# Turning the state columns of several chunks to rows with one transpose each: a two-layer decoder step on one Trainium2 core

## The chip, the cores and the metric

The kernel runs on one core of a Trainium2 chip, in one launch. The metric is the device time of one execution in microseconds; a median of several runs is given. The engines are called as in the profile: PE (TensorE; PEld is its weight load), DVE (VectorE), ACT (ScalarE), POOL (GpSimd) and SP (SyncE, which here only issues DMAs).

## What is computed

One inference step of two layers over 512 new prompt rows and 8 sequences of 4 decode rows, 544 rows in all, in float32. Layer 0 mixes tokens by a convolution module, layer 1 by stick-breaking attention; each layer ends in a feed-forward block with a gate that is convolved over 3 rows. Cut to what the change touches:

```python
D_MODEL, SEQ, DEC_BATCH, DEC_SEQ = 1024, 512, 8, 4
D_FF, CONV_WIDTH, FFN_CONV_WIDTH = 2816, 31, 3

def conformer_conv(h, past, ...):
    a, gate = jnp.split(h @ w_in + b_in, 2, axis=-1)
    glu = a * jax.nn.sigmoid(gate)
    ext = jnp.concatenate([past, glu], axis=1)
    y = causal_dwconv(ext, w_dw, b_dw)
    y = jax.nn.silu(layer_norm(y, ln_g, ln_b))
    return y @ w_out + b_out, ext[:, -(CONV_WIDTH - 1):]

def conv_ffn(h, past, w_gate, w_up, w_dw, b_dw, w_down):
    g = h @ w_gate
    ext = jnp.concatenate([past, g], axis=1)
    g_conv = causal_dwconv(ext, w_dw, b_dw)
    out = (jax.nn.silu(g_conv) * (h @ w_up)) @ w_down
    return out, ext[:, -(FFN_CONV_WIDTH - 1):]
```

The second results are outputs of the kernel, the states for the next step. The convolution's state is the last 30 rows of `glu` for the prompt, and for each decode sequence its 26 newest past rows and its 4 new ones, 1024 channels each. The feed-forward state is the last 2 rows of the gate for the prompt and for each of the 8 sequences, 18 rows of 2816 channels in each layer.

## The kernel before

Activations lie transposed: channels on the 128 partitions in chunks (8 chunks of the model's 1024 channels, 22 of the feed-forward's 2816), rows along the free axis. So a state that is to be written as rows has to be turned. A float32 product is made of three PE matmuls on rounded parts: weights split into `whi` and `wlo` (ACT casts, L369; DVE subtracts, L372), inputs into high and low parts (`XH`/`XL`, or `HH`/`HL` for the hidden layer of the feed-forward block). The first 272 or 256 rows and the rest are separate streams.

Each stage is written as a list of operations in `Plan`, with an engine, an assumed cost and the buffers read and written. `Plan.run` simulates them and so fixes the order of instructions on every engine; on the chip each engine runs its own list in order and waits where data are not there. Buffers are rings: a tile can be taken again when its last user is done. PSUM has eight banks, `acc` four, `tr` and `av` two each.

**Feed-forward block, `ffn` (once a layer).** The 22 chunks are taken in four passes, `PASSES = ((0, 4), (4, 6), (10, 6), (16, 6))` (first chunk, count). A pass makes gate products (into `acc` banks, emptied by ACT and DVE into a buffer `G`, two in a ring), convolves and multiplies with the up products, and leaves the pass's hidden chunks in `HH` and `HL`. The down products of a pass (L1343 to L1345, added to `xT` on DVE at L1634) run among the gate products of the next pass; those of the last pass follow the block (L459 to L461). `taps` has POOL copy a chunk's 18 state columns from `G` to `SF[:, f, :]` (L1491, L1492). When a pass ends, `state_rows` takes up to four chunks at a time: one PE transpose each (L1645) into one PSUM bank, side by side as [18, 128 x chunks], one ACT copy (L1652) to a tile of the ring `h` (four tiles, used for hidden chunks too), and two stores on POOL's queue, 2 rows of the prompt and 16 of the decode sequences (L1648, L1649). `psum2` takes the banks `tr` and `av` in turn.

**Convolution.** `state(False)` turns the last 30 prompt rows, which lie in `tail_p` [128, 8 chunks, 30], `state(True)` the 32 new decode rows in `glu_s` [128, 8, 32]: for each half of four chunks four transposes (L1117) into an `av` bank and one ACT copy (L1120) into a tile `prod` (two in a ring, which `ffn_rows` fills next). SP stores the prompt's rows with one DMA (L1128) and the decode rows with eight (L1126). Around them in the plan stand the last products of the convolution's output (L700 to L702), whose result DVE adds to `xT` (L1196), ACT squares (L1177) and POOL or DVE sums (L1184); L1207 turns that sum into a mean on PE.

## Time and profile before

| | |
|---|---|
| median of 3 runs | 1292.23 us (1292.02 to 1292.42) |
| profiled execution | 1294.01 us |
| its span on the core | 1292.0 us |
| clock granted to PE over the span | 0.998 of full |
| DMA engines' packets | 142.39 MB, mean 110 GB/s |

The page lists busy time by engine, then 40 slices of the span, then the chain that ended last, then the costliest groups. Each line of the timeline view has start, duration, engine, line of the kernel, operation, output and inputs, shapes and count; in brackets stand the idle time of the engine just before and what ended it. Matmul durations are latencies of pipelined instructions; successive ones overlap, so prices are read from the distance between starts.

The stages of the span, from the view by windows (busy us of PE, DVE and ACT):

| stretch, us | PE | DVE | ACT |
|---|---|---|---|
| 200 to 260 (end of convolution, start of block 0) | 59.86 | 45.98 | 31.63 |
| 260 to 640 (block 0, start of attention) | 377.18 | 294.42 | 189.52 |
| 640 to 900 (attention) | 258.14 | 168.30 | 160.96 |
| 900 to 1280 (block 1, final norm) | 379.02 | 301.41 | 195.79 |

### The profile page before, as it was taken

The numbers are of one execution on the slowest core, as the hardware profiler recorded it, in microseconds if no ns is written. First come the engines' busy times: TensorE is split into PE (matmuls) and PEld (weight loads), VectorE is DVE, ScalarE is ACT, GpSimd is POOL, SyncE is SP. The second block draws the span as 40 slices with busy tenths as digits, with TensorE's granted clock in tenths as the row PEclk, the third lists the DMA queues.
The fourth block names the chain that finished last, engine by engine and source line by source line (L and its number), as shares of the span: only waits on it lengthen the run. The fifth ranks groups of instructions, "written<-read, shape, count | busy, mean of one in ns | idle before, by whom it ended". The sixth has DMA issues, their size and how long they took to land.

```text
span 1292.0 us, 26645 instructions
## 1 busy us (share of the span) xinstructions
PE 1274.7 (99%) x10908; PEld 1220.0 (94%) x10908; DVE 981.1 (76%) x1671; ACT 718.5 (56%) x1448; POOL 158.5 (12%) x301
## 2 busy tenths in 40 slices
PE   9999999999999999999999999999999999999997
PEld 8997789999999999999988988889999999999997
DVE  6899876988977887768356586756988987886864
ACT  6596574545654455445356587754645655455453
POOL 4000013111011010000142123100111011011000
PEclk9999999999999999999999999999999999999999
DMA  7464333123233233143544446333133233233221
GB/s 214 123 184 134 88 99 114 34 83 115 91 106 102 83 99 115 58 141 135 180 148 130 139 129 175 110 116 98 50 100 101 92 105 115 66 116 92 81 76 70
DMA packets 119308, 142.39 MB, mean 110 GB/s; under 512 B 5588, under 2 KB 110312, under 8 KB 118915
## 3 DMA queue, kind: packets, MB, share of 16 engines
q1 hardware_dynamic: 109871, 111.89, 28.0%
q0 software_dynamic: 9024, 28.78, 7.2%
q8 instruction: 86, 1.41, 0.5%
q14 instruction: 35, 0.29, 0.1%
q10 hardware_dynamic: 292, 0.02, 0.0%
HBM read 129.34 MB, written 12.18 MB: 110 GB/s over the span
## 4 chain that ended last, share of the span: by engine, by line
PE 92%; DVE 3%; issue 2%; ACT 1%; DMA 1%; DVEq 0%; POOL 0%; ACTq 0%; POOLq 0%; SPq 0%
PE acc L1545 5%; PE acc L1543 5%; PE acc L1544 5%; PE acc L700 4%; PE acc L701 4%; PE acc L702 4%; PE av L1343 3%; PE acc L460 3%; PE acc L459 3%; PE acc L461 3%; PE av L1344 3%; PE av L1345 3%; PE tr L1343 3%; PE tr L1344 3%; PE tr L1345 3%; PE tr L1545 3%
## 5 line engine op out<-in xcount | busy, mean ns | idle before, releaser
L372 DVE TENSOR_TENSOR wlo<-raw,whi 128x1024 fp32r<-128x1024 f32 (+2 forms) x245 | 257.4, 1052 | 45.0 <-ACT whi L369 43.2
L369 ACT CAST whi<-raw 128x1024 fp32r<-128x1024 f32 (+2 forms) x245 | 223.5, 914 | 115.3 <-PE tr L1344 21.7
L700 PE MATMUL acc<-XH,whi 128*128 128x288 f32 (+1 forms) x384 | 114.4, 298 | 0.0
L701 PE MATMUL acc<-XL,whi 128*128 128x288 f32 (+1 forms) x384 | 110.8, 288 | 0.0
L702 PE MATMUL acc<-XH,wlo 128*128 128x288 f32 (+1 forms) x384 | 110.3, 287 | 0.0
L1970 PE MATMUL acc<-XH,whi 128*128 128x256 f32 (+1 forms) x264 | 82.8, 314 | 0.6 <-ACT XH L2275 0.6
L1543 PE MATMUL acc<-TH,whi 128*128 128x272 f32 x288 | 82.9, 288 | 0.0
L1545 PE MATMUL acc<-TH,wlo 128*128 128x272 f32 x288 | 82.8, 288 | 0.0
L1544 PE MATMUL acc<-TL,whi 128*128 128x272 f32 x288 | 82.7, 287 | 0.0
L1579 ACT COPY G<-acc 128x272 f32<-128x272 f32 (+1 forms) x72 | 26.7, 371 | 95.2 <-PE acc L1545 95.2
L1971 PE MATMUL acc<-XL,whi 128*128 128x256 f32 (+1 forms) x264 | 76.2, 289 | 0.1
L1972 PE MATMUL acc<-XH,wlo 128*128 128x256 f32 (+1 forms) x264 | 75.9, 287 | 0.0
L700 PEld LDWEIGHTS acc<-XH,whi 128*128 128x128 f32 x384 | 72.3, 188 | 2.8 <-issue 1.6
L1343 PE MATMUL av<-HH,whi 128*128 128x288 f32 (+1 forms) x256 | 74.5, 291 | 0.0
L1344 PE MATMUL av<-HL,whi 128*128 128x288 f32 (+1 forms) x256 | 74.1, 290 | 0.0
L1345 PE MATMUL av<-HH,wlo 128*128 128x288 f32 (+1 forms) x256 | 73.9, 289 | 0.0
L1343 PE MATMUL tr<-HH,whi 128*128 128x256 f32 (+1 forms) x256 | 73.4, 287 | 0.0
L1344 PE MATMUL tr<-HL,whi 128*128 128x256 f32 (+1 forms) x256 | 73.3, 286 | 0.0
L1345 PE MATMUL tr<-HH,wlo 128*128 128x256 f32 (+1 forms) x256 | 72.9, 285 | 0.0
L701 PEld LDWEIGHTS acc<-XL,whi 128*128 128x128 f32 x384 | 72.3, 188 | 0.4
L702 PEld LDWEIGHTS acc<-XH,wlo 128*128 128x128 f32 x384 | 72.2, 188 | 0.0
L1484 DVE SCALAR_TENSOR_TENSOR cv<-G,fprm,cv 128x560 f32<-128x560 f32 x88 | 69.4, 796 | 0.5
(409 smaller groups left out, 4417.4 us busy)
## 6 DMA issues: line engine op xcount, KB each, us to landing
raw<-in_ffn_w_gate_dram SPq DMA_DIRECT2D x22, 1024.0 KB
raw<-in_ffn_w_up_dram SPq DMA_DIRECT2D x22, 1024.0 KB
raw<-in_ffn_w_down_dram SPq DMA_DIRECT2D x24, 768.0 KB
raw<-in_attn_w_qkv_dram SPq DMA_DIRECT2D x12, 1024.0 KB
raw<-in_conv_w_in_dram POOLq DMA_DIRECT2D x6, 1024.0 KB, 6.3
rep<-glu SPq DMA_DIRECT2D x36, 142.0 KB
raw<-in_conv_w_out_dram POOLq DMA_DIRECT2D x4, 1024.0 KB, 6.3
raw<-in_ffn_w_down_dram SPq DMA_DIRECT2D x8, 512.0 KB
```

Source lines behind the costliest of these rows:

```text
L369: act.copy(hi[:, k, :], src[:, k])
L372: dve.tensor_tensor(lo[:, k, :], src[:, k], hi[:, k, :], op=ALU.subtract)
L700: pe.matmul(o, hi[:, k, :], XH[:, k, c0:c0 + n], start=(k == 0), stop=False)
L701: pe.matmul(o, hi[:, k, :], XL[:, k, c0:c0 + n], start=False, stop=False)
L702: pe.matmul(o, lo[:, k, :], XH[:, k, c0:c0 + n], start=False, stop=(k == NC - 1))
L1343: pe.matmul(o, hi[:, j + k, :], xh, start=(start and k == 0), stop=False, **kw)
L1344: pe.matmul(o, hi[:, j + k, :], xl, start=False, stop=False, **kw)
L1345: pe.matmul(o, lo[:, j + k, :], xh, start=False, stop=(stop and k == len(xs) - 1), **kw)
L1543: pe.matmul(o, hi[:, j + k, :], xh, start=(start and k == 0), stop=False, **kw)
L1544: pe.matmul(o, hi[:, j + k, :], xl, start=False, stop=False, **kw)
L1545: pe.matmul(o, lo[:, j + k, :], xh, start=False, stop=(k == 3), **kw)
L1970: pe.matmul(o, hi[:, k, :], XH[:, k, c0:c0 + n], start=(k == 0), stop=False)
```

## The change

A transpose turns [128 partitions, n columns] to [n, 128]. The new code lets the n columns be those of several chunks that lie side by side. In the feed-forward block a pass's part of `SF` (18 x 4 or 18 x 6 columns) is filled in the order row by row, within a row chunk by chunk (`mine`), so one transpose gives [72 or 108, 128], with the 2 prompt rows' pieces first. One ACT copy of 128 elements a partition follows, and two stores of pieces of 128 channels. There are no smaller groups any more: one PSUM bank, one tile `h`, one copy and two stores a pass. In the convolution four chunks of `tail_p` (120 columns) or `glu_s` (128 columns) are turned at once, the two halves into one bank, side by side; one ACT copy of 256 elements takes both, and four DMAs on SP store them, one for each place of a chunk within its half.

```diff
@@ -1107,26 +1107,24 @@
 
     def state(new):
         m = NS if new else PAST
-        row = buf("ctmp", "prod", [P, D], 2)
-        for half in range(2):
-            pt = psum("av")
-
-            def turn(half=half, pt=pt):
-                for j in range(4):
-                    c = half * 4 + j
-                    pe.transpose(pt()[:m, j * P:(j + 1) * P], glu_s[:, c, :] if new else tail_p[:, c, :], ident)
-
-            plan.op("pe", 0.45, turn, r=[("new" if new else "tail", half * 4 + j) for j in range(4)], w=[pt])
-            plan.op("act", 0.56, lambda half=half, pt=pt: act.copy(row()[:m, half * 512:(half + 1) * 512], pt()[:m, :]),
-                    r=[pt], w=[row])
+        src = (glu_s if new else tail_p).rearrange("p c t -> p (c t)")
+        row, pt = buf("ctmp", "prod", [P, D], 2), psum("av")
+
+        def turn():
+            for half in range(2):
+                pe.transpose(pt()[:4 * m, half * P:(half + 1) * P], src[:, 4 * half * m:4 * (half + 1) * m], ident)
 
         def store():
-            if new:
-                for b in range(NB):
-                    nc.sync.dma_start(out=sc_s[0, b, PAST - NI:PAST, :], in_=row()[b * NI:(b + 1) * NI, :])
-            else:
-                nc.sync.dma_start(out=sc_p[0, 0], in_=row()[:m, :])
-
+            for j in range(4):
+                r = row()[j * m:(j + 1) * m, :2 * P].rearrange("t (h d) -> t h d", h=2)
+                if new:
+                    dst = sc_s[0, :, PAST - NI:PAST, :].rearrange("b t (h j d) -> b t h j d", h=2, j=4)
+                    nc.sync.dma_start(out=dst[:, :, :, j, :], in_=r)
+                else:
+                    nc.sync.dma_start(out=sc_p[0, 0].rearrange("t (h j d) -> t h j d", h=2, j=4)[:, :, j, :], in_=r)
+
+        plan.op("pe", 0.22, turn, r=[("new" if new else "tail", c) for c in range(NC)], w=[pt])
+        plan.op("act", 0.33, lambda: act.copy(row()[:4 * m, :2 * P], pt()[:4 * m, :2 * P]), r=[pt], w=[row])
         plan.op("sp", 3.0, store, r=[row])
 
 
@@ -1488,9 +1486,11 @@
             plan.op("act", 0.2, lambda: act.activation(
                 smp(s(), SEQ, T), s()[:, SEQ:].rearrange("p (b t) -> p b t", b=NB)[:, :, 2:], AF.Silu), r=["table"], w=[s])
             gs = lambda: g()[:, 2 + SEQ:].rearrange("p (b t) -> p b t", b=NB)
-            plan.op("pool", 0.2, lambda: pool.tensor_copy(SF[:, f, 0:2], g()[:, SEQ:SEQ + 2]), r=[g], w=[("SF", f)])
+            k0, nk = next(x for x in PASSES if x[0] <= f < sum(x))
+            mine = SF[:, k0:k0 + nk, :].rearrange("p f r -> p (f r)").rearrange("p (r f) -> p f r", f=nk)[:, f - k0, :]
+            plan.op("pool", 0.2, lambda: pool.tensor_copy(mine[:, 0:2], g()[:, SEQ:SEQ + 2]), r=[g], w=[("SF", f)])
             plan.op("pool", 0.2, lambda: pool.tensor_copy(
-                SF[:, f, 2:18].rearrange("p (b t) -> p b t", b=NB), gs()[:, :, 4:6]), r=[g], w=[("SF", f)])
+                mine[:, 2:18].rearrange("p (b t) -> p b t", b=NB), gs()[:, :, 4:6]), r=[g], w=[("SF", f)])
 
         def plain_pair(f2, s0, k0):
 
@@ -1636,22 +1636,21 @@
                 used(slots[c - c2])
 
         def state_rows(k0, nk):
-            for f0 in range(k0, k0 + nk, 4):
-                m = min(4, k0 + nk - f0)
-                pt, row = psum2(), buf(None, "h", [P, T], H_BUFS)
-
-                def turn(f0=f0, m=m, pt=pt):
-                    for j in range(m):
-                        pe.transpose(pt()[:18, j * P:(j + 1) * P], SF[:, f0 + j, :], ident)
-
-                def store(f0=f0, m=m, row=row):
-                    pool.dma_start(out=sf_p[l, 0][:, f0 * P:(f0 + m) * P], in_=row()[0:2, :m * P])
-                    pool.dma_start(out=sf_s[l].flatten_outer_dims()[:, f0 * P:(f0 + m) * P], in_=row()[2:18, :m * P])
-
-                plan.op("pe", 0.11 * m, turn, r=[("SF", f0 + j) for j in range(m)], w=[pt])
-                plan.op("act", acost(m * P), lambda m=m, pt=pt, row=row: act.copy(row()[:18, :m * P], pt()[:18, :m * P]),
-                        r=[pt], w=[row])
-                plan.op("pool", 1.4, store, r=[row])
+            pt, row = psum2(), buf(None, "h", [P, T], H_BUFS)
+            m = 18 * nk
+
+            def store():
+                r = row()[:m, :P]
+                fs = slice(k0 * P, (k0 + nk) * P)
+                for dst, lo, n in ((sf_p[l, 0], 0, 2), (sf_s[l].flatten_outer_dims(), 2, 16)):
+                    pool.dma_start(out=dst[:, fs].rearrange("r (f c) -> r f c", f=nk),
+                                   in_=r[lo * nk:(lo + n) * nk])
+
+            plan.op("pe", 0.11, lambda: pe.transpose(
+                pt()[:m, :P], SF[:, k0:k0 + nk, :].rearrange("p f r -> p (f r)"), ident),
+                r=[("SF", f) for f in range(k0, k0 + nk)], w=[pt])
+            plan.op("act", acost(P), lambda: act.copy(row()[:m, :P], pt()[:m, :P]), r=[pt], w=[row])
+            plan.op("pool", 1.4, store, r=[row])
 
 
         first = slot_no[0]
```

The planner sees other costs and fewer operations, so some orders move. On PE, at the end of the convolution, the rows around the state transposes (av, tr, acc: PSUM banks; sqa: the sum of squares). Before:

```order
L1117 MATMUL av_178_2647<-ident_61,tail_p_84 30x128 x4
L1117 MATMUL av_179_2654<-ident_61,tail_p_84 30x128 x4
L700 MATMUL acc_182_2666<-XH_73,whi16_1444 128x288
L701 MATMUL acc_182_2666<-XL_74,whi16_1444 128x288
L702 MATMUL acc_182_2666<-XH_73,wlo16_1445 128x288
...
L1207 MATMUL tr_183_2676<-sqa_166_2483,mean_m_66 128x256
L1117 MATMUL av_184_2680<-ident_61,glu_s_88 32x128 x4
L1117 MATMUL av_186_2689<-ident_61,glu_s_88 32x128 x4
```

and now:

```order
L1115 MATMUL av_178_2647<-ident_61,tail_p_84 120x128 x2
L1115 MATMUL av_179_2651<-ident_61,glu_s_88 128x128 x2
L700 MATMUL acc_183_2667<-XH_73,whi16_1444 128x288
L701 MATMUL acc_183_2667<-XL_74,whi16_1444 128x288
L702 MATMUL acc_183_2667<-XH_73,wlo16_1445 128x288
...
L1205 MATMUL tr_184_2682<-sqa_166_2483,mean_m_66 128x256
```

The transposes of `glu_s` moved from behind the mean of squares (L1207, in the new kernel L1205) to the place beside those of `tail_p`, ahead of the same six matmuls (three are shown).

On ACT, at the end of the feed-forward block of layer 0 (h: ring of rows and hidden chunks; raw, whi: weights; sqa: the next norm's squares). Before:

```order
L369 CAST whi131_7009<-raw47_6892 128x768
L1596 CAST HH0_3038<-h_395_6906 128x544
L1652 COPY h_401_7026<-av_399_7017 18x512
L1652 COPY h_402_7029<-tr_400_7022 18x256
L369 CAST whi132_7034<-raw48_6963 128x768
L1596 CAST HH0_3038<-h_397_6942 128x544
```

and now:

```order
L369 CAST whi131_6969<-raw47_6852 128x768
L1596 CAST HH0_3021<-h_389_6866 128x544
L1652 COPY h_394_6979<-av_393_6977 108x128
L369 CAST whi132_6986<-raw48_6923 128x768
L1596 CAST HH0_3021<-h_391_6902 128x544
```

The two copies became one at the same place, between the casts of the last two hidden chunks.

On POOL, where the second pass of layer 0 ends (out_3 and out_7: the two feed-forward states). Before:

```order
L1461 COPY G_291_4452<-fprm_76 128x8x2
L1461 COPY G_299_4620<-fprm_76 128x8x2
L1648 DMA out_3_dram<-h_307_4810 2x512
L1649 DMA out_7_dram<-h_307_4810 16x512
L1648 DMA out_3_dram<-h_308_4813 2x256
L1649 DMA out_7_dram<-h_308_4813 16x256
L1491 COPY SF0_3040<-G_291_4452 128x2
L1492 COPY SF0_3040<-G_291_4452 128x16
```

and now:

```order
L1459 COPY G_289_4432<-fprm_76 128x8x2
L1459 COPY G_297_4600<-fprm_76 128x8x2
L1646 DMA out_3_dram<-h_304_4784 2x6x128
L1646 DMA out_7_dram<-h_304_4784 16x6x128
L1491 COPY SF0_3023<-G_289_4432 128x2
L1492 COPY SF0_3023<-G_289_4432 128x16
```

Four stores became two, with the same copies ahead and behind. Apart from such places the order of PE is the same in both kernels; in the feed-forward block the names of the banks `tr` and `av` change places.

## The prediction

> **What bounds the kernel now.** I read the page first: the busy shares, then the chain of work that ended last.
>
> ```profile
> span 1292.0 us, 26645 instructions
> ...
> PE 1274.7 (99%) x10908; PEld 1220.0 (94%) x10908; DVE 981.1 (76%) x1671; ACT 718.5 (56%) x1448; POOL 158.5 (12%) x301
> ...
> PE 92%; DVE 3%; issue 2%; ACT 1%; DMA 1%; DVEq 0%; POOL 0%; ACTq 0%; POOLq 0%; SPq 0%
> ```
>
> TensorE (PE) is busy 1274.7 of 1292.0 us and holds 92% of the chain. So an instruction taken off PE is worth its issue interval, unless what stands behind it in PE's fixed order has to wait for something else. Two questions follow: what does one of the removed transposes cost, and what stands behind each of them.
>
> Second view, the two lines that the change rewrites (min/median/max ns, first and last start, forms):
>
> ```profile
> L1645 PEld LDWEIGHTS av<-ident,SF x28: 89/91/92, 270.2 to 1239.2; 128*18 128x18 f32 x28
> L1645 PE MATMUL av<-ident,SF x28: 271/273/273, 270.3 to 1239.3; 128*18 128x128 f32 x28
> ...
> L1645 PE MATMUL tr<-ident,SF x16: 270/272/273, 365.6 to 1239.6; 128*18 128x128 f32 x16
> ```
>
> ```profile
> L1117 PE MATMUL av<-ident,tail_p x8: 271/272/273, 191.4 to 192.2; 128*30 128x128 f32 x8
> ...
> L1117 PE MATMUL av<-ident,glu_s x8: 272/272/273, 193.8 to 194.5; 128*32 128x128 f32 x8
> ```
>
> 44 transposes of 18 columns run in the feed-forward layers and 16 in the convolution. The 272 ns is the latency of one; they overlap. The price is the distance between starts, read from the timeline of PE around the convolution's state rows:
>
> ```profile
> 191.42 1.03 PE L1117 MATMUL av<-ident,tail_p 128*30 128x128 f32 x8
> 192.21 0.38 PE L700 MATMUL acc<-XH,whi 128*128 128x288 f32 x1
> ...
> 193.22 0.70 PE L1207 MATMUL tr<-sqa,mean_m 128*128 128x256 f32 x2
> 193.76 1.04 PE L1117 MATMUL av<-ident,glu_s 128*32 128x128 f32 x8
> ...
> 194.77 0.29 PE L701 MATMUL acc<-XL,whi 128*128 128x288 f32 x1
> 194.90 0.30 PE L702 MATMUL acc<-XH,wlo 128*128 128x288 f32 x1
> ```
>
> The eight transposes of glu_s start at 193.76; the first product behind them is followed by its second matmul at 194.77, and a 288-column matmul takes 0.13 us of PE (194.77 to 194.90). So eight cost 194.77 - 193.76 - 0.13 = 0.88 us, **0.11 us each** (0.109 to 0.110).
>
> **The change, part by part.** Feed-forward: each layer has four passes, of 4, 6, 6 and 6 chunks, and one transpose a pass in place of one a chunk. 22 become 4: 18 fewer a layer, 36 in all, 3.9 us at 0.109. Convolution: 16 become 4, 12 fewer, 1.3 us. If all of it lay on PE's path, 5.2 us would go. The order of PE is otherwise the same in both kernels, so three places decide.
>
> (1) *Is one wide transpose as cheap as one narrow one?* The moving operand stays the 128x128 identity; the stationary one grows from 18 columns to 72 or 108 (120 and 128 in the convolution). The nearest rows are the final norm's transposes, whose stationary operand has 128 columns and which stand as pairs between products:
>
> ```profile
> 1245.10 0.38 PE L1741 MATMUL yt<-ident,xg 128*128 128x128 f32 x2
> 1245.23 0.36 PE L459 MATMUL acc<-HH,whi 128*128 128x256 f32 x1
> 1245.43 0.29 PE L460 MATMUL acc<-HL,whi 128*128 128x256 f32 x1
> ```
>
> ```profile
> L1741 PEld LDWEIGHTS yt<-ident,xg x40: 95/139/144, 1245.0 to 1284.5; 128*128 128x128 f32 x32, 128*32 128x32 f32 x8
> ```
>
> The load takes 139 ns there against 91 ns for 18 columns, but the pair costs 1245.43 - 1245.10 - 0.12 (a 256-column matmul, 1239.80 to 1239.92 below) = 0.21 us, 0.105 each: the longer load hides behind the matmul before. I take 0.11 for a wide one. The other bound is that the load's extra 48 ns shows each time: 12 wide transposes, 0.6 us lost.
>
> [...]
>
> (2) *The passes that are followed by more work.* At the first three boundaries of each layer PE goes from products of one kind to products whose inputs were made long before; no wait of PE stands there. 3 + 5 + 5 transposes fewer are worth 13 x 0.109 = 1.42 us a layer, **2.83 us** for both. ACT's copies shrink too (of 512 and 256 elements to 128), and POOL issues two stores instead of four; neither is on the path there, so I price them at nothing.
>
> (3) *The end of each layer.* Here the transposes fill PE while the last two chunks of the hidden layer (HH, HL) are finished. PE, then ACT, then DVE, in layer 1 (layer 0 looks the same at 558):
>
> ```profile
> 1239.02 0.60 PE L1645 MATMUL av<-ident,SF 128*18 128x128 f32 x4
> 1239.46 0.38 PE L1645 MATMUL tr<-ident,SF 128*18 128x128 f32 x2
> 1239.60 0.36 PE L459 MATMUL acc<-HH,whi 128*128 128x256 f32 x1
> 1239.80 0.28 PE L460 MATMUL acc<-HL,whi 128*128 128x256 f32 x1
> 1239.92 0.28 PE L461 MATMUL acc<-HH,wlo 128*128 128x256 f32 x1
> ...
> 1241.34 0.28 PE L461 MATMUL acc<-HH,wlo 128*128 128x256 f32 x1
> 1241.89 0.38 PE L459 MATMUL acc<-HH,whi 128*128 128x256 f32 x1 [0.27 <-ACT HH L1596]
> 1242.97 0.39 PE L460 MATMUL acc<-HL,whi 128*128 128x256 f32 x1 [0.70 <-DVE HL L1597]
> ```
>
> ```profile
> 1239.71 0.58 ACT L1652 COPY h<-av 18x512 f32<-18x512 f32 x1 [0.61 <-PE av L1645]
> 1240.20 0.36 ACT L1652 COPY h<-tr 18x256 f32<-18x256 f32 x1
> 1240.46 0.83 ACT L369 CAST whi<-raw 128x768 fp32r<-128x768 f32 x1
> 1241.19 0.64 ACT L1596 CAST HH<-h 128x544 fp32r<-128x544 f32 x1
> ```
>
> ```profile
> 1240.23 0.71 DVE L1597 TENSOR_TENSOR HL<-h,HH 128x544 fp32r<-128x544 f32 x1
> 1241.32 0.96 DVE L372 TENSOR_TENSOR wlo<-raw,whi 128x768 fp32r<-128x768 f32 x1 [0.38 <-ACT whi L369]
> 1242.20 0.72 DVE L1597 TENSOR_TENSOR HL<-h,HH 128x544 fp32r<-128x544 f32 x1
> ```
>
> Six transposes take 1239.80 - 1239.02 - 0.12 = 0.66 us, and five fewer bring PE to its sixth chunk 0.55 earlier. But it already waits there: 0.27 us for HH and 0.70 for HL. So ask what moves HL. It is the last of: transposes, two copies on ACT, the weight cast L369, the weight split L372 on DVE, HL. The copy starts 0.36 us after the fourth transpose (1239.02 + 3 x 0.109 = 1239.35); behind a lone transpose it starts at 1239.38. Copies start the next instruction 0.49 us (512) and 0.26 us (256) later, so 128 elements take about 0.15, and the cast starts near 1239.53 instead of 1240.46, 0.93 earlier. DVE can't use all of that: it is busy with the fifth chunk's HL until 1240.23 + 0.71 = 1240.94 and idle only the 0.38 us after it. So the split, HL and PE's 1242.97 move by 0.38, a little more if issue overlaps; I take 0.40. HH is no limit, since its cast follows the weight cast by 0.73. An end is worth **0.40**, both 0.80 (bounds for each: nothing, if ACT's part stayed; 0.93, what the weight cast moves, if DVE's run were earlier too). What is late next is DVE's own run of work.
>
> (4) *Convolution.* In the new order both pairs of transposes stand ahead of six matmuls and then the mean of squares L1207. That mean waits for a chain that has nothing to do with the transposes:
>
> ```profile
> 191.62 0.48 DVE L1196 SCALAR_TENSOR_TENSOR xT<-acc,prm,xT 128x256 f32<-128x256 f32 x1 [0.25 <-PE acc L702]
> 192.02 0.82 DVE L904 TENSOR_TENSOR XL<-ext_p,XH 128x288 fp32r<-128x288 f32 x2
> 192.75 0.42 DVE L1184 TENSOR_TENSOR sqa<-sq,sqa 128x256 f32<-128x256 f32 x1
> ```
>
> ```profile
> 192.19 0.42 ACT L1177 ACTIVATE sq<-xT 128x256 f32<-128x256 f32 x1 [0.70 <-DVE xT L1196]
> ```
>
> xT at 191.62, its square at 192.19, the sum at 192.75 which ends at 193.17, and the mean starts at 193.22, the moment the sum is there. The change leaves all three where they are. So PE, done with four transposes (0.44) and six matmuls (0.80) at about 192.66, idles until 193.22: what is saved ahead of the mean (four transposes' worth) is given back. Behind it the eight transposes of glu_s are gone: **0.88 us**. The second XL (in the pair that starts at 192.02) ends about 192.46 and is asked for near 192.4; that wait lies in the same hole. Bounds: 0.44 (a cast of XH or XL late behind the mean) and 1.31 (the mean's chain moves too). The stores become 4 + 4 DMAs on SP for 1 + 8, with pieces of 512 B; they are ready earlier than before, and what is queued behind them on SP, the loads of ffn_rows, goes out no later. Nothing.
>
> Sum: 2.83 + 0.80 + 0.88 = **4.5 us**. The profiled execution has a span of 1292.0 within 1294.01 us; the median of the runs shown is 1292.23, 1.8 below that execution. So the span goes to 1287.5, the median to 1292.23 - 4.5 = **1287.7 us**, 0.35% faster.
>
> Also moved: the additions of the first down products on DVE (L1634) change places with each other, in the order in which PE finishes them, and one G memset falls behind two weight splits; G's second half is written much later than that. Nothing. POOL writes SF with a stride; the same elements, nothing.
>
> **The rivals.**
> *All of it counts* (12%): waits at the ends and in the convolution shrink along with PE's work, because DVE's run ahead of the end starts earlier too. For it: that run is fed by PE. Against it: the mean's chain. 5.2 us, up to 2.83 + 1.86 + 1.31 = 6.0 with both upper bounds: 1286.2 to 1287.0.
> *The waits take it* (11%): the ends give nothing, the convolution 0.44 and the wide loads show 0.6 at their worst: 2.83 + 0.44 - 0.6 = 2.7, 1289.5. For it: PE does wait in both places. Against: ACT's two copies stand in the very chain that it waits for.
> *It does not do what it says* (6%): PE is only the fullest engine, and its order is paced by others, so that time saved turns into waits later on, and a third of it stays: 1.5 us, 1290.7. Against: 92% of the chain.
> *Slower* (5%): POOL. One pass's rows leave as 108 pieces of 512 B in two stores instead of four stores of 18 and 2 rows, and behind those stores in POOL's queue stand the copies G to SF, which free the two G buffers, into which ACT empties PE's accumulators.
>
> ```profile
> 369.51 0.51 POOL L1649 DMA_DIRECT2D out_dram<-h  x1
> 370.81 0.18 POOL L1491 COPY SF<-G 128x2 f32<-128x2 f32 x1 [0.79 <-ACT G L1579]
> ```
>
> ```profile
> L332 POOL DMA_DIRECT2D raw<-in_conv_w_out_dram x4: 882/882/884, 86.9 to 162.3; - x4
> ```
>
> If a store's issue cost went by pieces, at 50 ns a piece the six boundaries with 108 pieces would hold POOL 5.4 us each. The four stores of before take 4 x 0.51 = 2.05, and POOL then idles 0.79 until 370.81, so 2.8 us are free. Beyond that every us could reach PE: 2.6 x 6 = 15.6 us, 1292.2 - 4.5 + 15.6 = 1303. It turns slower than before at 2.8 + 4.5/6 = 3.6 us, 33 ns a piece. Against it: a 1 MB load, 128 partitions of 8 pieces, issues in 0.88 us, under 1 ns a piece.
>
> **How the numbers follow.** The forecast has 66%, with a range of its own of 1287.0 to 1288.7 (5.2 us off; and 2.83 + 0.80 + 0.44 - 0.6 = 3.5 us off, with the convolution and the loads at their low bounds). The range that should hold the time 8 times in 10 takes in the first two rivals: 1286.4 to 1289.6. What this measurement can tell from no change is about 0.2%, 2.6 us. Forecast, first rival and nearly all of the second are faster by more: 0.88. The third, and the rest of the second, lie within: 0.07. Slower: 0.05.
>
> **What would show it.** Right: eight lone transposes in the feed-forward blocks and four in the convolution, 48 fewer on PE; no new wait of PE at the first three boundaries; at each layer's end the copy on ACT about 0.25 us long, the wait for HL about 1.1 instead of 0.70, that for HH smaller; in the convolution a new wait of PE of about 0.4 us for the sum L1184, and the product behind the mean starting near 193.76. Wrong: a distance of over 0.15 us behind a wide transpose; a wait of PE for G or XH; POOL stores that last over 2 us; a gain under 2.6 or over 6.0 us.

## The result, and the profile after

| | before | changed |
|---|---|---|
| median of 8 runs | 1292.36 us | 1289.39 us |
| lowest and highest | 1292.02, 1294.52 us | 1287.61, 1290.49 us |
| ratio, 95% interval | | 0.9972 (0.9961 to 0.9983) |
| profiled execution, its span | 1294.01, 1292.0 us | 1289.36, 1287.7 us |

The changed kernel is faster by 0.28% (0.17 to 0.39%), some 3.6 us. First its page, as for before: span, busy shares, and the shares of the chain that ended last.

```profile
span 1287.7 us, 26497 instructions
...
PE 1270.2 (99%) x10860; PEld 1215.5 (94%) x10860; DVE 980.4 (76%) x1671; ACT 713.5 (55%) x1440; POOL 152.4 (12%) x289
...
PE 85%; DVE 10%; issue 2%; ACT 1%; DMA 1%; DVEq 0%; POOL 0%; ACTq 0%; POOLq 0%
```

The 48 matmuls that the change removes are gone (10908 to 10860). The chain reads otherwise: PE has 85% of it instead of 92, DVE 10% instead of 3. That is the trace of the one place where the prediction failed, shown below: in the two experiments that take the wait away there (e1 and e12) PE has 91% again and DVE 4%.

The sum is best checked by distances within one execution, because the executions differ in their first 17 us by up to 1.9 us, in no order that follows the kernels (last section). The landmarks are the starts of the state transposes in PE's timeline (tail_p, then the boundary of each pass, the fourth being the layer's end) and of the mean-of-squares product of the stage behind each layer (L577 behind layer 0, L1759 or L1760 behind layer 1):

| distance, us | before | changed | less | predicted |
|---|---|---|---|---|
| tail_p to layer 0, first boundary | 191.42 to 270.32: 78.90 | 190.15 to 268.17: 78.02 | 0.88 | 0.88 |
| first to second | to 365.65: 95.33 | to 363.56: 95.39 | -0.06 | 0.33 |
| second to third | to 465.69: 100.04 | to 463.06: 99.50 | 0.54 | 0.55 |
| third to fourth | to 558.19: 92.50 | to 555.01: 91.95 | 0.55 | 0.55 |
| fourth to the mean of the next stage | to 580.94: 22.75 | to 577.28: 22.27 | 0.48 | 0.40 |
| layer 1, first to second | 951.19 to 1046.48: 95.29 | 948.73 to 1044.04: 95.31 | -0.02 | 0.33 |
| second to third, third to fourth | 100.04, 92.50 | 99.50, 91.95 | 0.54, 0.55 | 0.55, 0.55 |
| fourth to the mean of the final norm | 1239.02 to 1272.05: 33.03 | 1235.49 to 1268.07: 32.58 | 0.45 | 0.40 |

Together 3.91 us where 4.54 were predicted. All terms but one are within 0.08 of their value; the first boundary gives nothing in either layer. What stands there, in PE's timeline of the changed kernel:

```profile
268.17 0.27 PE L1649 MATMUL av<-ident,SF 128*72 128x128 f32 x1
...
274.19 0.27 PE L1343 MATMUL tr<-HH,wlo 128*128 128x256 f32 x1
274.60 0.40 PE L1341 MATMUL av<-HH,whi 128*128 128x288 f32 x1
274.83 0.29 PE L1342 MATMUL av<-HL,whi 128*128 128x288 f32 x1
```

The down product into `av` should start at 274.31 (274.19 and 0.12 for a 256-column matmul). It starts at 274.60, 0.29 us late (the view puts no bracket on it), and its second matmul follows 0.23 us later where 0.13 is usual. DVE's timeline at that place:

```profile
272.75 0.69 DVE L1314 TENSOR_TENSOR raw<-S,raw 128x512 f32<-128x512 f32 x1
273.48 0.69 DVE L1316 TENSOR_TENSOR raw<-raw 128x512 f32<-128x512 f32 x1
274.09 0.45 DVE L1634 TENSOR_TENSOR xT<-av,xT 128x288 f32<-128x288 f32 x1
```

The kernel has two `av` banks. The product that starts at 274.60 takes the bank which the add L1634 of 274.09 empties, and that add is the end of a run in which DVE has no idle time over 0.04 us. The view of the chain now goes back through that run without naming another engine, from 274.1 to the reciprocal of the norm at 226.34 (start, length, engine, output and line; first and last piece):

```profile
226.34 1.96 DVE rstd L1372
...
273.48 0.69 DVE raw L1316
```

In the kernel before, PE came to the same product three transposes later and started it without delay (PE, then DVE):

```profile
276.66 0.28 PE L1345 MATMUL tr<-HH,wlo 128*128 128x256 f32 x1
276.77 0.35 PE L1343 MATMUL av<-HH,whi 128*128 128x288 f32 x1
276.96 0.30 PE L1344 MATMUL av<-HL,whi 128*128 128x288 f32 x1
```

```profile
276.21 0.81 DVE L1634 TENSOR_TENSOR xT<-av,xT 128x288 f32<-128x288 f32 x2
```

In the changed kernel the product starts 274.60 - 274.09 = 0.51 us behind the add's start; by that, the bank of before was free for PE at 276.21 + 0.51 = 276.72, and PE came at 276.77. It had 0.05 us to spare, or less: its second matmul follows 0.19 us later, where 0.13 is usual. The change brings PE 0.33 earlier, measured from the boundary, and doesn't bring the add earlier: that starts 276.21 - 270.32 = 5.89 us behind the boundary before and 274.09 - 268.17 = 5.92 now.

At the end of a layer, PE, ACT and DVE in layer 1:

```profile
1235.49 0.27 PE L1649 MATMUL av<-ident,SF 128*108 128x128 f32 x1
1237.47 0.39 PE L460 MATMUL acc<-HL,whi 128*128 128x256 f32 x1 [0.17 <-DVE HL L1597]
1238.97 0.38 PE L460 MATMUL acc<-HL,whi 128*128 128x256 f32 x1 [0.88 <-DVE HL L1597]
```

```profile
1235.85 0.27 ACT L1652 COPY h<-av 108x128 f32<-108x128 f32 x1 [0.27 <-PE av L1649]
1236.20 0.84 ACT L369 CAST whi<-raw 128x768 fp32r<-128x768 f32 x1
1236.94 0.64 ACT L1596 CAST HH<-h 128x544 fp32r<-128x544 f32 x1
```

```profile
1236.70 0.72 DVE L1597 TENSOR_TENSOR HL<-h,HH 128x544 fp32r<-128x544 f32 x1
1237.33 0.95 DVE L372 TENSOR_TENSOR wlo<-raw,whi 128x768 fp32r<-128x768 f32 x1
1238.20 0.72 DVE L1597 TENSOR_TENSOR HL<-h,HH 128x544 fp32r<-128x544 f32 x1
```

One copy of 0.27 us stands where two were; the weight cast follows, HH is no longer waited for, and PE waits 0.17 and 0.88 us for HL. DVE runs through without the 0.38 us of idle time that it had.

### The profile page after: what moved, and what is told of

Read it like the earlier page. It is cut to its first block, busy times and chain, and to the rows that moved or that the text cites. A ratio compares the mean times of both kernels' runs of the same rounds, so it can differ in the third digit from the quotient of the medians.

```text
span 1287.7 us, 26497 instructions
## 1 busy us (share of the span) xinstructions
PE 1270.2 (99%) x10860; PEld 1215.5 (94%) x10860; DVE 980.4 (76%) x1671; ACT 713.5 (55%) x1440; POOL 152.4 (12%) x289
## 4 chain that ended last, share of the span: by engine, by line
PE 85%; DVE 10%; issue 2%; ACT 1%; DMA 1%; DVEq 0%; POOL 0%; ACTq 0%; POOLq 0%
PE acc L1545 5%; PE acc L1543 5%; PE acc L1544 5%; PE acc L700 4%; PE acc L701 4%; PE acc L702 3%; PE acc L459 3%; PE acc L460 3%; PE acc L461 3%; PE tr L1544 3%; PE tr L1543 3%; PE tr L1545 3%; PE av L1341 3%; PE acc L1969 3%; PE av L1343 3%; PE av L1342 3%
## 5 line engine op out<-in xcount | busy, mean ns | idle before, releaser
L1341 PE MATMUL av<-HH,whi 128*128 128x288 f32 x256 | 76.2, 298 | 0.2
L1342 PE MATMUL av<-HL,whi 128*128 128x288 f32 x256 | 75.5, 295 | 0.0
L1343 PE MATMUL av<-HH,wlo 128*128 128x288 f32 x256 | 75.3, 294 | 0.0
L1341 PE MATMUL tr<-HH,whi 128*128 128x256 f32 x256 | 71.9, 281 | 0.0
L1342 PE MATMUL tr<-HL,whi 128*128 128x256 f32 x256 | 71.9, 281 | 0.0
L1343 PE MATMUL tr<-HH,wlo 128*128 128x256 f32 x256 | 71.5, 279 | 0.0
```

What stands on the lines that cost most here:

```text
L1341: pe.matmul(o, hi[:, j + k, :], xh, start=(start and k == 0), stop=False, **kw)
L1342: pe.matmul(o, hi[:, j + k, :], xl, start=False, stop=False, **kw)
L1343: pe.matmul(o, lo[:, j + k, :], xh, start=False, stop=(stop and k == len(xs) - 1), **kw)
```

## The experiments

Of each edit the lines that matter are shown. Distances are taken as above. Those of the changed kernel repeat well: in the second execution that was profiled (e6, below) all those of the table lie within 0.06 us of the first.

**e1: the narrow transposes back at the first boundary alone.**

```diff
 def state_rows(k0, nk):
+    if nk == 4:
+        return narrow_rows(k0, nk)
```

> The changed kernel with the four narrow transposes put back at the first boundary of each feed-forward layer (the pass of 4 chunks) alone; all else as changed. Theory (DVE's add L1634, which frees the PSUM bank of the down product, comes when DVE's own unbroken run of work is done, about 5.9 us behind the boundary, and PE's product into that bank waits for it): PE comes 0.33 us later to that product and finds the bank free, so the distance from the first to the second boundary of a layer stays where it is in the changed kernel, 95.39 us in layer 0 and 95.31 in layer 1, within 0.05, and the wait of 0.3 us ahead of the product into av near 274.6 is gone. Rival (the three transposes less were worth their 0.11 us each on PE, and something else took as much back later in the pass): the distance grows by 0.33 us, to 95.7.

`narrow_rows` is the code of before. Measured: 267.90 to 363.24, 95.34 us, and 95.31 in layer 1. PE's timeline at the product:

```profile
274.23 0.27 PE L1343 MATMUL tr<-HH,wlo 128*128 128x256 f32 x1
274.35 0.36 PE L1341 MATMUL av<-HH,whi 128*128 128x288 f32 x1
```

Four transposes or one make no difference here, and the product starts 0.12 us behind the one before. So the three transposes' worth is spent in waiting, not lost further on.

**e2: the adds ahead of the second raw sum, by priority.**

```diff
 plan.op("dve", dcost(n), lambda ...: dve.tensor_tensor(x, pt()[:, :n], x, op=ALU.add),
-        r=[pt], w=[("x", c, h)])
+        r=[pt], w=[("x", c, h)], urgent=FIRST_ADDS[c != c2] if nk == 4 else 0.0)   # (6.0, 1.0)
```

> The changed kernel with one thing moved: on DVE the two adds of the down product into av (L1634) come ahead of the second raw sum (L1316) at the first boundary, not behind it. The add that frees the bank ends about 0.25 to 0.3 us earlier. Theory (DVE's add is late): the wait of PE of 0.3 us at the first boundary falls to under 0.1 and the distance from the first to the second boundary falls from 95.39 to about 95.1 us in layer 0 and from 95.31 to about 95.05 in layer 1; 0.55 us for both layers. Rival (DVE is the bound of that whole pass, so that what is gained at its head is lost again at the raw sum that is now later): the wait goes, but the distance stays at 95.3 to 95.4.

Measured: 269.24 to 364.17, 94.93 us, and 94.93 in layer 1: 0.46 and 0.38 less than the changed kernel. The expectation says that one thing was moved; that was not so. The priority holds for all adds of that pass, and the planner also put other adds earlier and one group of PE's products elsewhere. e12 makes the same test without that.

**e12: only the second raw sum moved, behind the first adds.**

```diff
 plan.op("dve", dcost(512), lambda: dve.tensor_tensor(
     W.raw[r][:, 4:, 0:P], W.raw[r][:, 0:4, 0:P], W.raw[r][:, 4:, 0:P], op=ALU.add), r=[first], w=[("S2", r)],
+    after=[lead.pop()] if lead else ())   # lead: the first add of the first down product of a 4-chunk pass
```

> The changed kernel with the second raw sum (L1316) put behind the first adds at the first boundary on DVE (here both adds of av and the first of tr), and nothing else moved: PE's order, and DVE's from there on, are those of the changed kernel, while the early adds of the earlier run had also moved further adds and one group of products on PE. Theory (the add that frees the bank is all that PE waits for there): from the wide transpose to the first product into the freed bank 6.43 us becomes 6.13, and the distance from the first to the second boundary 95.39 and 95.31 become 95.05 to 95.1 in layer 0 and 95.0 in layer 1; what the earlier run gained beyond 0.30 (0.16 and 0.08) belongs to its other moves and is not seen here. Rival (the pass as a whole is bound by DVE): 95.3.

```profile
274.32 0.27 PE L1344 MATMUL tr<-HH,wlo 128*128 128x256 f32 x1
274.44 0.30 PE L1342 MATMUL av<-HH,whi 128*128 128x288 f32 x1
274.57 0.29 PE L1343 MATMUL av<-HL,whi 128*128 128x288 f32 x1
```

```profile
272.88 0.69 DVE L1314 TENSOR_TENSOR raw<-S,raw 128x512 f32<-128x512 f32 x1
273.49 0.81 DVE L1635 TENSOR_TENSOR xT<-av,xT 128x288 f32<-128x288 f32 x2
274.58 0.68 DVE L1316 TENSOR_TENSOR raw<-raw 128x512 f32<-128x512 f32 x1
```

Measured: the first product into the freed bank starts 6.13 us behind the transpose (268.31 to 274.44), as expected. The second boundary is at 363.32, 95.01 us behind the first, and 94.94 in layer 1: 0.38 and 0.37 less than the changed kernel, a little more than the 0.30 of the wait (against e6, e9 and e11, which have the same boundary, 0.31 to 0.33 and 0.36 to 0.37). The order of PE and of ACT is that of the changed kernel; on DVE two memsets of `G` of 0.06 us moved with the sum. The remainder fits the matmul behind the wait, which in the changed kernel takes 0.23 us until the next starts, here 0.13. On this kernel's page PE has 91% of the chain and DVE 4%. With the transposes taken off, the distance is now 95.01 - 0.11 = 94.90, and in the kernel before 95.33 - 4 x 0.11 = 94.89: before, DVE's add cost nothing there.

**e3: HL of the last chunk ahead of the weight split.**

```diff
 if slot == last_slot():
     held.append(split_low)          # DVE's half of the split, created later
...
     i = plan.op("dve", dcost(T), lambda: dve.tensor_tensor(HL[:, f - k0, :], ...))
+    if f == NF - 1:
+        while held:
+            held.pop()((i,))        # split behind this HL
```

> The changed kernel with one thing moved: at the end of each feed-forward layer DVE makes HL of the last chunk (L1597) ahead of the weight split wlo (L372) that stood ahead of it. Theory (what is late there now is DVE's own run of work, the split in it): HL starts when its HH is cast, about 557.0 instead of 557.72 in layer 0, PE's wait for HL falls from 0.88 us to about 0.2, and each layer's end gets 0.65 to 0.75 us shorter (from the last boundary to the output stage 37.15 to about 36.45, and 37.49 to about 36.8), 1.3 to 1.5 us in all. Rival (the split is wanted as soon, since it is the fifth weight of the next product): the wait for HL goes, and one for wlo of about as much takes its place four products later; the time stays.

```profile
1235.89 0.72 DVE L1608 TENSOR_TENSOR HL<-h,HH 128x544 fp32r<-128x544 f32 x1
1236.88 0.73 DVE L1608 TENSOR_TENSOR HL<-h,HH 128x544 fp32r<-128x544 f32 x1 [0.27 <-ACT HH L1607]
1237.52 0.95 DVE L372 TENSOR_TENSOR wlo<-raw,whi 128x768 fp32r<-128x768 f32 x1
```

```profile
1236.66 0.39 PE L460 MATMUL acc<-HL,whi 128*128 128x256 f32 x1 [0.17 <-DVE HL L1608]
1237.66 0.39 PE L460 MATMUL acc<-HL,whi 128*128 128x256 f32 x1 [0.38 <-DVE HL L1608]
```

Measured: from the last boundary to the output stage 556.21 to 592.75, 36.54 us (0.61 less), and in layer 1 1234.69 to 1271.65, 36.96 (0.53 less); to the mean of the next stage 21.65 and 32.05. The 1.14 us are somewhat under the 1.3 to 1.5 expected, because HL now waits 0.27 us for its HH on ACT. No wait for the split took its place. So what was late last at the layer's end was DVE's own run, the split in it.

**e7: the same move in the kernel before.**

> The kernel before with HL of the last chunk ahead of the weight split at each layer's end, the narrow transposes left. Theory (the last HL waits for two things in turn, ACT's cast HH, which stands behind the two copies of the transposes and the weight cast, and DVE's split): with the split out of the way HL starts when HH is cast, and here HH comes late, since the copies hold ACT: HL at 1241.85 instead of 1242.20, 0.35 us a layer, PE's wait for HL from 0.70 to about 0.35; the layer end 37.63 to about 37.3. In the changed kernel the same move gave 0.61 and 0.53. Rival (only DVE's run counts, the copies on ACT are hidden): the same 0.6 as in the changed kernel.

Measured, to the mean of the next stage: 556.53 to 578.95, 22.42 us instead of 22.75, and 32.71 instead of 33.03, 0.33 and 0.32 less. HL now waits 0.93 us for HH, which stands behind the two copies and the weight cast on ACT:

```profile
1238.14 0.72 DVE L1608 TENSOR_TENSOR HL<-h,HH 128x544 fp32r<-128x544 f32 x1
1239.79 0.73 DVE L1608 TENSOR_TENSOR HL<-h,HH 128x544 fp32r<-128x544 f32 x1 [0.93 <-ACT HH L1607]
```

So both parts of the chain are real: ACT's copies delay HH, DVE's split delays HL, and the change frees only the first.

**e4: the convolution's tail_p alone.**

> The kernel before with the wide transposes in the convolution for tail_p alone (two for eight); glu_s keeps its eight, and the feed-forward layers keep theirs. In this order all ten stand ahead of the mean of squares. Measured from the first transpose of tail_p to the first boundary of the feed-forward layer, 78.90 us in the kernel before and 78.02 in the changed one. Theory (the mean waits for DVE's sum, whatever the transposes do, so what counts is what stands behind the mean): the eight of glu_s, moved ahead of it, fill the hole that PE would idle in, and PE is done at about 193.3, just as the sum is there: 0.79 us less, 78.1, though only six transposes are gone. Rival (each transpose taken off PE counts, wherever it stands): 6 x 0.109 = 0.65 us less, 78.25. Rival (what is saved there is lost): 78.9.

Measured: 190.21 to 269.00, 78.79 us, 0.11 less than before; the theory said 0.79, so the rival in which the saving is lost came nearest. Up to the mean it held: the second matmul of the product behind the mean starts 192.85 - 190.21 = 2.64 us behind tail_p, against 194.77 - 191.42 = 3.35 before, 0.71 earlier. The rest was lost within 7 us, to XL:

```profile
198.70 0.29 PE L700 MATMUL acc<-XH,whi 128*128 128x288 f32 x1
199.34 0.40 PE L701 MATMUL acc<-XL,whi 128*128 128x288 f32 x1 [0.35 <-DVE XL L904]
```

```profile
195.57 1.92 DVE L904 TENSOR_TENSOR XL<-ext_p,XH 128x288 fp32r<-128x288 f32 x2
198.30 0.99 DVE L904 TENSOR_TENSOR XL<-ext_p,XH 128x288 fp32r<-128x288 f32 x1
```

```profile
191.31 1.03 ACT L1120 COPY prod<-av 32x512 f32<-32x512 f32 x2
192.25 0.76 ACT L903 CAST XH<-ext_p 128x288 fp32r<-128x288 f32 x2
193.29 1.09 ACT L903 CAST XH<-ext_p 128x288 fp32r<-128x288 f32 x3
```

The two copies of glu_s (the pair at 191.31) now stand ahead of ACT's casts XH, two XH come before the root of the norm (`rstd`, 192.92) and three after it, and DVE makes one XL only at 198.30, when PE is waiting for it. In the changed kernel the copy takes 0.36 us, four XH are cast ahead of the root, and that wait is not there. So the whole 0.88 us seems to need the shorter copies too, which have no term in the prediction's sum (only its low bound, 0.44, has a cast of XH or XL late behind the mean); a kernel that differs from the changed one in long copies alone was not tried. This kernel also lost 0.64 us in layer 1 (951.85 to 1047.79, 95.94 us from first to second boundary, 95.29 before), partly to a wait of PE for ACT near the end of that pass; why is not known.

**e8: the convolution's half alone.**

> The kernel before with the convolution's half of the change alone (tail_p and glu_s in two wide transposes each), the feed-forward layers as before. Theory: from the first transpose of tail_p to the first boundary 78.90 us becomes 78.02, 0.88 less, and nothing else moves: 0.9 us less than the kernel before. Rival (as the two wide transposes of tail_p alone showed, a lead at the mean is lost again to XL on DVE): 0.1 to 0.3.

Measured: 190.15 to 268.17, 78.02 us, 0.88 less; the other distances are those of the kernel before (95.32, 100.04, 92.50). The ratio of the runs' times is 0.9994 (0.9985 to 1.0003): the effect is too small for them to tell, not for the distances in the trace.

**e11: five wide transposes for one at two boundaries of layer 0.** Four of them only repeat the first.

> The changed kernel with five wide transposes in place of one at the second and the third boundary of layer 0 (four of them only repeat it). Theory (a wide transpose costs PE 0.109 us, as a narrow one): the distances that begin there, 99.50 and 91.95 us, grow by 0.44 each to 99.94 and 92.39. By the rival of the prediction's bound, in which the longer weight load of a wide one shows (48 ns more each): 0.63 each, 100.13 and 92.58. On the dip behind the attention: PE comes there 0.9 us later than in the changed kernel. If the dip depends on when the idle times fall, its share (9 of 16 runs of the changed kernel at a clock of 0.997 or less) changes; if it belongs to the code there, the share stays about half.

```profile
364.50 0.71 PE L1653 MATMUL av<-ident,SF 128*108 128x128 f32 x5
...
464.44 0.71 PE L1653 MATMUL av<-ident,SF 128*108 128x128 f32 x5
...
556.84 0.27 PE L1653 MATMUL av<-ident,SF 128*108 128x128 f32 x1
```

Measured: 99.94 and 92.40 us. Four more cost 0.44 and 0.45: 0.11 us for a wide transpose, behind another wide one too.

**e5 and e6: both moves together, beside the changed kernel.**

> The changed kernel with both moves together: the two adds of the down product ahead of the second raw sum at the first boundary, and HL of the last chunk ahead of the weight split at each layer's end. Theory (two waits at different places, each PE's own): the gains add up, 0.46 + 0.38 at the first boundaries and 0.61 + 0.53 at the ends, 2.0 us less than the changed kernel timed beside it; the undisturbed runs near 1285.6. Rival (what one frees the other loses, since both only push DVE's work later): 1.1 us or less. On the dip of the granted clock behind the attention (856 to 866 us in the changed kernel's profile, none in the profile of before, of the changed kernel with narrow rows at the first boundary and of the two kernels with one move): if it comes and goes with the execution, runs of this kernel, of the changed one and of the kernel before fall apart into levels 1.5 to 2 us apart in about the same shares; if it belongs to the changed kernel, that one alone does.

> The changed kernel, unaltered, beside the others of this call. From the local distances of its profile 4.0 us less than the kernel before (0.88 in the convolution, 0.54 + 0.55 + 0.48 in layer 0, 0.54 + 0.55 + 0.45 in layer 1). If the dip of the clock comes with the execution, the profile of this repeat may be free of it, and the distance from the second mean of the attention layer's norm (598.89) to the next block's (888.27) is then near 287.9 instead of 289.38; if it belongs to the kernel, it is there again at the same place.

| same chip | median | lowest and highest | ratio to before, 95% interval |
|---|---|---|---|
| before, 18 runs | 1293.08 us | 1291.43, 1293.91 | |
| changed, 8 runs | 1289.11 us | 1287.65, 1290.47 | 0.9973 (0.9962 to 0.9983) |
| both moves, 5 runs | 1285.90 us | 1285.57, 1286.39 | 0.9946 (0.9932 to 0.9959) |

The gains add up: first to second boundary 94.93 and 94.99 us, layer ends 21.65 and 32.04, so 0.46 + 0.32 + 0.62 + 0.54 = 1.9 us by distances; lowest to lowest 2.1. This kernel is faster than the changed one and than the one before, by 0.54%. e6, the changed kernel, shows no dip behind the attention (599.15 to 887.01, 287.86 us), so the same code has it in one execution and not in another.

**e9 and e10: PE kept busier at the end of the attention.** Eight transposes of ident that nothing reads are added in PE's idle time there.

```diff
 products([u], 0.82e-3 * 2 * sum((i + 1) * P for i, _ in UNITS[u]), (av, u))
+if u != 1:
+    fill = psum("t")
+    plan.op("pe", 0.44, busy, r=[(av, u)], w=[fill], urgent=50.0)   # four transposes of ident
```

> The changed kernel with PE kept busier at the end of the attention: four transposes of ident into a free bank are added behind the first products of the last pair (where PE stands still 0.69 us in the changed kernel, 855.5 to 856.19), and four behind the last ones (ahead of the 0.61 us at 858.00). Nothing reads them; 0.44 us each, less than either wait. Theory (the granted clock falls to 0.50 for about 3.4 us behind these idle times in some executions, because PE was little used there, and that is what spreads the changed kernel's runs over 1287.6 to 1290.5 us): the dip does not come, no run shows a clock of 0.997 or less for the execution, and all runs lie at 1287.5 to 1289.0 (the loads at the start, which come up to 1.3 us earlier or later, remain). Rival (the dip has another cause, or comes whatever PE does there): about half of the runs show it still, at 1289 to 1290.5, and the eight added transposes cost up to 0.2 us.

> The two moves (adds ahead of the second raw sum, HL ahead of the weight split) with the same eight transposes. Theory: these moves take 2.0 us off the changed kernel, and its five runs showed no dip already (1285.57 to 1286.39, clock 0.998 each), so nothing more is to be had: 1285.6 to 1286.5. Rival (the eight transposes lie on PE's path, since each wait there is followed by products that were waited for): 0.3 to 0.9 us slower than without them.

Measured: e9 1287.59 to 1289.24 us in five runs, e10 1285.66 to 1287.70; no run at a clock of 0.997 or less. Both theories gave a somewhat narrower range than came out (to 1289.0 and to 1286.5). The eight transposes cost next to nothing (e9 599.81 to 887.70, 287.89 us, with 287.86 in e6; e10 599.40 to 887.33, 287.93, with 287.78 in e5). But e11, which leaves those idle times as they were and only comes there 0.9 us later, shows no such run in six either, so the theory of e9 isn't shown by it.

## Why the prediction was right, and where not

The forecast was 1287.7 us in a range of 1286.4 to 1289.6, and faster; measured were 1289.39, within it and near its upper end, but above the 1287.0 to 1288.7 that the forecast gave for itself; in the second set of runs the change is worth 4.0 us, which is inside. The rival in which the waits take the gain gave 1289.5, but it isn't what happened: its ends gave nothing and its convolution 0.44, where 0.45 to 0.48 and 0.88 were measured.

- *Price of a wide transpose, 0.11.* Right. PEld shows the longer loads of the eight lone transposes:

```profile
L1649 PEld LDWEIGHTS av<-ident,SF x8: 113/128/129, 268.0 to 1235.4; 128*108 128x108 f32 x6, 128*72 128x72 f32 x2
```

113 to 129 ns against 91 for a narrow one, hidden behind the matmul before, as e11's 0.11 each says. The bound of 0.6 us lost can go.

- *The passes followed by more work, 2.83.* **Here the step failed.** It held for the second and third boundary (0.54 and 0.55, predicted 0.55). For the first it said "no wait of PE stands there", and took the 0.33 us per layer as gained. There was none because PE came just in time: DVE's unbroken run sets the moment at which the bank is free, and PE had 0.05 us to spare. So 0.65 of the 2.83 us turned into a new wait for the add L1634. The step had looked for waits in the trace of before, not for how long before PE's arrival each bank was free.
- *The ends, 0.80.* Right in mechanism, 0.93 measured. The copy is 0.27 us, but the weight cast starts 0.35 us behind it (1235.85, 1236.20), not the 0.15 that was expected; that changed nothing, since DVE's run was later. The waits for HL come to 1.05 us together (1.1 were expected), that for HH is gone. e3 and e7 show both halves of the chain. With the split out of the way in both kernels the change is worth 22.42 - 21.65 = 0.77 us at the end of layer 0 and 32.71 - 32.05 = 0.66 in layer 1, instead of 0.48 and 0.45: what is late next was DVE's own run, as predicted.
- *The convolution, 0.88.* The distance is exact, and what is saved ahead of the mean is given back as said: PE waits for the sum. (The row at 191.25 starts 0.14 us late, for XL; that lies in the same hole, as foreseen.)

```profile
190.15 0.38 PE L1115 MATMUL av<-ident,tail_p 128*120 128x128 f32 x2
191.25 0.40 PE L701 MATMUL acc<-XL,whi 128*128 128x288 f32 x1
191.96 0.70 PE L1205 MATMUL tr<-sqa,mean_m 128*128 128x256 f32 x2 [0.17 <-DVE sqa L1182]
192.62 0.29 PE L701 MATMUL acc<-XL,whi 128*128 128x288 f32 x1
```

190.15 to 192.62 is 2.47 us; before, 191.42 to 194.77 was 3.35. The reason given for it was incomplete: by e4, a lead at the mean can be lost again to XL. One argument of this step was wrong without harm. The eight stores hold SP for 3.87 + 2.90 us, where the nine of before took 0.37 + 2.68, so the loads behind them go out 198.00 - 190.15 = 7.85 us behind `tail_p` instead of 198.28 - 191.42 = 6.86: later, not "no later".
- *POOL's stores.* No price by pieces was seen; the 50 ns a piece of the slower rival was assumed, and no run shows it. In a pass of six chunks they have 12 and 96 pieces; at the second boundary these two took 0.56 and 0.54 us to issue, all sixteen 0.52 to 0.64 (0.51 to 0.57 before), so the slower rival falls:

```profile
L1646 POOL DMA_DIRECT2D out_dram<-h x16: 520/559/637, 270.3 to 1237.0; - x16
```

- *POOL's copies to `SF`.* Priced at nothing; with the stride those of 16 columns (L1492) take 213 ns in the median, 197 before.
- *From distances to the median.* The changed kernel's distances come to 3.9 us; the medians differ by 3.0 in the first set and by 4.0 in the second, the ratios say 3.6 and 3.5. In the changed kernel's first profile 1.5 us went to a dip of the clock, the next section's; the lowest runs are 4.4 us apart in the first set and 3.8 in the second.

## What to carry to other kernels

Before an instruction's time on the fullest engine is taken as gained, look for the next place where that engine meets another one, and read how long before the meeting the other is done; a wait that isn't in the trace may have been missed by 0.05 us. An engine that is without a gap for tens of microseconds (DVE here, in both kernels, for 48 us ahead of the add) can be the next bound, though the chain doesn't name it. Where such a meeting is found, moving the awaited instruction ahead of its neighbours in its engine's order was worth as much here (1.9 us for two moves) as half of the change itself.

## What the runs showed of the hardware

**The clock behind the attention.** In the changed kernel's profile the granted clock falls to half for 3.4 us (1.0 + 2.0 + 0.4 by the three rows below full speed; in stretches of 0.2 us the view has 0.50 in each from 859.0 to 862.2, 0.96 and 0.51 in the one ahead and the one behind, and 1.00 on both sides of these), right behind the idle times of PE at the end of the attention (the view by windows; the column ahead of the last two is the clock):

```profile
856.00:858.00 2.00, 1.21 (x11) 0.83 (x11) 0.44 (x3) 0.70 (x3) 0.00 (x0) 1.00 0.00 0
858.00:860.00 2.00, 1.86 (x9) 1.66 (x10) 0.89 (x3) 0.42 (x1) 0.00 (x0) 0.75 0.00 0
860.00:862.00 2.00, 2.00 (x12) 2.00 (x11) 0.86 (x3) 0.42 (x1) 0.00 (x0) 0.50 0.00 0
862.00:864.00 2.00, 2.00 (x16) 2.00 (x16) 1.08 (x3) 0.83 (x2) 0.00 (x0) 0.90 0.00 0
```

The distance from the second mean of the attention layer's norm to that of the next block is 289.38 us there (598.89 to 888.27) and 287.86 in the repeat. Of the other profiled executions only e4's shows it (0.52 and 0.62 in the two stretches of 2 us from 862 to 866; by these an estimate of 3.4 us, if it stood at 0.50), behind the same place. Over all timed runs of the changed kernel 9 of 16 have a mean clock of 0.997 or less; of the kernel before 1 of 18 on one chip and 4 of 10 on another; of e8 1 of 11; of e5, e9, e10 and e11 none of 21. A mean doesn't tell where the clock fell (the profiles of both kernels also end at 0.50 once PE is done: from 1287 us in the kernel before, from 1283 in the changed one), but it fits: the two profiles with the dip have 0.997, the twelve others 0.998 or 0.999. No run shows what sets it off. The longest idle time of PE in the 20 us ahead of the dip is 0.69 us, and PE is busy for 1.21 of the 2 us from 856; the same waits, 0.69 and 0.61 us, stand in the profile of before (ahead of the products at 860.17 and 861.98), and its clock is 1.00 from 850 to 868 us. Why the same code meets the dip in some executions only, and why the changed kernel met it so often, stays open.

**The start.** tail_p's transposes start between 189.76 and 191.58 us in the fourteen profiles of this study, in no order that follows the kernels (190.15 and 190.47 for the changed one). The difference is there by 17 us: the first product with mean_m starts between 15.06 and 16.92 us. In the changed kernel and e3 it is at 15.42 and 16.75, and 1.3 us of difference stay to 190.15 and 191.40.

**A wait cost more than its length.** Behind the 0.29 us at 274.60 the first matmul takes 0.23 us to the next, not the 0.13 of 274.44 to 274.57 in e12 (0.23 or 0.24 in both layers of e6, e9 and e11 too), and e12 got 0.31 to 0.38 back.
